# Shifting the starts of split weight parts and letting two PSUM banks take turns in a float32r decoder layer

## Chip, cores and metric

The kernel runs on one core of one Trainium2 chip. The metric is the device time of one execution in microseconds (us), the median of several runs.

## The reference

One hybrid decoder layer in float32 on 256 tokens of 2048 features. Cut to what matters:

```python
x = x + 0.5 * swiglu(rms_norm(x, g1), gate1, up1, down1)     # 2048 -> 5632 -> 2048
x = gated_parallel_mixer(x, ...)    # p = rms_norm(x) @ w_in; windowed attention and RWKV-7;
                                    # sigmoid gates; two projections; w_out
x = memory_cross_attention(x, mem, ...)
x = x + 0.5 * swiglu(rms_norm(x, g2), gate2, up2, down2)
return rms_norm(x, final)

def swiglu(h, w_gate, w_up, w_down):
    return (silu(h @ w_gate) * (h @ w_up)) @ w_down
```

Nearly all arithmetic is the product of 256 rows of tokens with weight matrices that are each read once.

## The kernel before

**Products.** `weight_plan` lists 105 products in their order; `EDGES` marks where the mixer (34) and the second feed-forward (71) begin. A product takes all 256 tokens against 512 columns of a weight matrix (288 in one case) and sums over its rows in chunks of 128. The tokens are two blocks of 128, so a product has two PSUM banks, `o[0]` and `o[1]`, from three rotating buffers named `acc`. A feed-forward works through three groups of columns (4, 4 and 3 times 512). Within a group gate and up products alternate, and then come four down products whose input is `h`. From product 71 on, the odd ones are all eleven gate products and six of the twelve down products.

**Split operands.** Each float32 operand is kept as two float32r parts, `hi` and `lo`, that add up to it, and each chunk costs three matmuls per bank: activation high part times weight `hi` (line 336), high part times weight `lo` (line 337), activation low part times weight `hi` (line 338). The activation chunk is the stationary operand (128x128, loaded by a LDWEIGHTS before each matmul), the weight part is the moving one (512 columns). The names after `<-` in the profile are moving, then stationary: `acc<-lo,xhi`.

**Units.** Weights are loaded by SyncE and split in units of two chunks (`KU`), twelve matmuls to a unit: six into `o[0]`, then six into `o[1]`. `divide` makes `hi` by a cast on ScalarE (line 299) and `lo` by a subtraction on VectorE (line 300), two units ahead of the multiplication (`AHEAD`), from loads that run further ahead. `hi` and `lo` have three buffers each, so the cast for unit u + 2 waits until TensorE has finished unit u - 1.

**Places.** The stationary operands are `xhi`/`xlo` (the normalised input of the feed-forwards and of most mixer products), `hhi`/`hlo` (the feed-forwards' inner activations) and the mixer's `ya`, `yr`, `mt`, `me` and `oc`. Where a tile begins within each partition follows from the allocation, in order of declaration in steps of 32 bytes. Taken modulo 128 bytes, all buffers of `hi` and `lo` begin at 96, `xhi` and `xlo` at 96, `hhi` and `hlo` at 64, and the mixer's tiles at 0, 32, 64 or 96 by their slot, since slots are 4128 bytes apart. Chunks and token blocks within a tile are multiples of 512 bytes apart.

**Order.** Between the steps of a product the `Interleave` object emits short steps of other work (transposes, norms, the mixer's attention and recurrence) by `bg.tick()`. A scheduler then orders each engine's instructions and sets the waits. The banks of a gate product are emptied by ScalarE (SiLU, line 415), those of an up product by VectorE (line 418), those of a down product by VectorE (line 427).

Of the kernel before, what the change touches and what calls it, by code (L numbers as in the profile page):

```python
# [15 lines left out]
P = 128  # L16
T = 256
# [10 lines left out]
KU = 2  # L28
# The decayed query-side factors carry 2^-40, the masks and the carried state 2^40: no product
# of a later key with an earlier query, which the masks remove, can overflow.  # L30
UP, DOWN = 2.0**40, 2.0**-40
GROUPS = ((0, 4), (4, 4), (8, 3))
N4 = 20
# Weight units whose split, and whose load, runs ahead of the one that is multiplied.
AHEAD, LOADED = 2, 4
# Products before the mixer, and before the second feed-forward.
EDGES = (34, 71)


class Act:  # L40
    """Activations with features on partitions, as two float32r parts that add up to them."""

# [8 lines left out]
class Interleave:  # L51
    """Short steps of other work, traced between the steps of the weight products."""

# [35 lines left out]
def weight_plan(a):  # L89
    """Every product with a weight matrix in its order: matrix, row chunk, chunks, column, columns."""  # L90
    w = {n: v[0] for n, v in a.items() if "_w_" in n or n.startswith("w_")}
    yield from feed_forward_plan(w["ffn1_w_gate"], w["ffn1_w_up"], w["ffn1_w_down"])
    w_in = w["w_in"]
    cols = [0, 512, ATTN_W]
    for c in cols:
        yield w_in, 0, KD, c, 512
    yield w_in, 0, KD, C_RW + 3 * RW, 288
    for h in range(2):
        yield w_in, 0, KD, C_RW + RW + h * 512, 512
    for n in range(4):  # L100
        yield w_in, 0, KD, C_GATE + n * 512, 512
        yield w["w_proj_attn"], 0, 8, n * 512, 512
    for h in range(2):
        yield w_in, 0, KD, C_RW + h * 512, 512
        yield w_in, 0, KD, C_RW + 2 * RW + h * 512, 512
    for n in range(4):
        yield w_in, 0, KD, C_GATE + D + n * 512, 512
    for n in range(4):
        yield w["w_proj_rwkv"], 0, 8, n * 512, 512
    for n in range(4):  # L110
        yield w["w_out"], 0, KD, n * 512, 512
    yield w["w_cross_kv"], 0, KD, 0, 512
    yield w["w_cross_q"], 0, KD, 0, 512
    yield w["w_cross_kv"], 0, KD, 512, 512
    for n in range(4):
        yield w["w_cross_o"], 0, 4, n * 512, 512
    yield from feed_forward_plan(w["ffn2_w_gate"], w["ffn2_w_up"], w["ffn2_w_down"])
# [3 lines left out]
def decoder_layer(ctx: ExitStack, tc: tile.TileContext, a: dict, out: bass.AP):  # L121
# [37 lines left out]

# [1 line left out]
    ones = cpool.tile([P, P], F32, name="ones")  # L161
# [9 lines left out]
    select(ident[:], ones[:], [[-1, P]], ALU.is_equal, 0.0, 0, 1)  # L171
    # attention bias: [previous block | current block], rows are queries
    abias = cpool.tile([P, 2, P], F32, name="abias")
    pool.memset(abias[:], 0.0)
    select(abias[:, 0, :], abias[:, 0, :], [[1, P]], ALU.is_gt, NEG, 0, -1)
    select(abias[:, 1, :], abias[:, 1, :], [[-1, P]], ALU.is_ge, NEG, 0, 1)
    # masks with the source step on partitions and the later step along the row
    ups = cpool.tile([P, P], F32, name="ups")
# [4 lines left out]
    select(mask3[:, 2, :], ups[:], [[1, P]], ALU.is_ge, 0.0, 0, -1)  # L183
    # with the later step on partitions
    mask_l = cpool.tile([P, P], F32, name="mask_l")
# [20 lines left out]

# [1 line left out]
    def row_vectors(rows, name, queue):  # L208
        """The vectors, and what fills them once their rows are there."""
        n = len(rows)  # L210
        r = cpool.tile([n, P], F32, name=name + "_r")
        at = 0
        while at < n:
            src, lo = rows[at]
            m = 1
            while at + m < n and rows[at + m][0] is src and rows[at + m][1] == lo + m * P:
                m += 1
            queue.dma_start(
                r[at : at + m, :], src[lo : lo + m * P].rearrange("(c p) -> c p", p=P)
            )  # L220
            at += m
        v = cpool.tile([P, n], F32, name=name)

        def fill():
            t = tr()
            pe.transpose(t[:, :n], r[:], ident[:n, :n])
            return act.copy(v[:], t[:, :n])

        return v, fill
# [36 lines left out]

# [1 line left out]
    plan = list(weight_plan(a))  # L268
# [5 lines left out]
    def load(u):  # L274
        """In the feed-forwards two units at once, into the pool of that phase."""
        if u >= len(units) or u in raws:
# [14 lines left out]
    def divide(u):  # L291
        if u >= len(units) or u in parts:
            return
        n, raw = units[u][3], raws[u]
        hi = wp.tile([P, KU, n], F32R, tag="hi", name="hi")
        lo = wp.tile([P, KU, n], F32R, tag="lo", name="lo")
        for s in (slice(0, 1), slice(1, 2)) if u == 0 else (slice(0, KU),):
# [14 lines left out]
    def product(x: Act, w, skew=False):  # L312
        """Rows of tokens: two [128, n] banks of x.T @ (the next columns of w)."""
        pw, _, nk, _, n = plan[at["product"]]
# [4 lines left out]
        for k in range(0, nk - KU * len(skewed), KU):  # L319
            bg.until(lambda: all(k + i in x.done for i in range(KU)))  # L320
            u = next_unit()
            for t in range(2):
                multiply(o[t][:, :n], x, u, k, t, nk)
                bg.tick()
        last = [(k, next_unit()) for k in skewed]
        for t in range(2):
            for k, u in last:
                multiply(o[t][:, :n], x, u, k, t, nk)
        return o

    def multiply(o, x, u, k, t, nk):
# [8 lines left out]
    def feat(tok, cols):  # L340
        """Token rows [128, 2, n] -> at up to two column offsets [128, 2, T] with features on
        partitions."""
        b = tr()
# [6 lines left out]
    def split(x: Act, c, n, src):  # L350
        """src (float32, PSUM or SBUF) -> chunks c to c + n of x."""
        act.copy(x.at(0, c, n), src)  # L352
        dve.tensor_tensor(x.at(1, c, n), src, f32(x.at(0, c, n)), ALU.subtract)
        x.done |= set(range(c, c + n))

# [1 line left out]
    class Norm:  # L357
# [8 lines left out]
        def block(self, n, src):  # L366
            """Steps for column block n of 512, src [128, 2, 512]; the last one ends the sums."""
            for h in range(2):
# [28 lines left out]

# [1 line left out]
    def feed_forward(sp, x, norm: Norm, wg, wu, wd, done, last=False):  # L399
# [41 lines left out]

    # ==== feed-forward 1 ====
    with tc.tile_pool(name="f1", bufs=1, reuse_waits="tile") as sp:
# [28 lines left out]

    # ==== token mixer and cross attention ====
    with tc.tile_pool(name="mx", bufs=1, reuse_waits="tile") as sp:
# [17 lines left out]

        # -- attention: a group of heads and a block of queries at a time --
        def to_features(tok, dst, name):
# [14 lines left out]
        def keys_values():  # L509
            # keys of each of the four heads on both halves of the partitions  # L510
            b = feat(tok_kv, C4[:2])
# [88 lines left out]

        # -- RWKV: columns with token shift, features on partitions --
        def shifted(tok, cols, mus, outs, name):
# [35 lines left out]
        def decay_and_rate():  # L638
# [28 lines left out]
            for h in range(2):  # L667
# [15 lines left out]
                act.activation(dec[h][:], dec[h][:], AF.Exp, scale=-DECAY)  # L683
                # decay from the middle of a chunk to each step, after that to the step before it
                ee.append(t4("ee", (P, 8, P + 1)))
# [10 lines left out]
        def removal_keys(h):  # L696
# [39 lines left out]
            pool.tensor_tensor(aa[h][:], kt[h][:], ei[:], ALU.mult)  # L736
            # products of the removal keys of later with those of earlier steps: L
            for c in range(2):
# [20 lines left out]

        # (1 - D)^-1 of the 32-step diagonal blocks, one block per partition  # L760
        def substitute():
# [27 lines left out]

        # -- the attention branch, gated --  # L790
        for n in range(4):
# [8 lines left out]

        # -- RWKV: receptances and values --
        rt, vtok, bv = [], [], []
# [15 lines left out]
        def values(h):  # L818
# [3 lines left out]
            for c in range(2):  # L822
                b = tr()
                # the recurrence keeps, and the group norm wants, values less their mean in a head
                for j in range(4):
# [16 lines left out]

        # -- RWKV: the two chunks of a pair of heads --
        xb = {}
# [121 lines left out]

        # -- group norm, bonus, gate, for two pairs --
        yr = Act([], [], 4)
# [53 lines left out]

        # -- the gate of the RWKV branch --
        for n in range(4):
# [5 lines left out]

        # -- merge and project out --
        mt = act_tiles("mt", 4)
# [38 lines left out]

        # -- cross attention --
        km, vm, qc = t4("km"), t4("vm", (P, 2, 512)), t4("qc")
# [68 lines left out]

    # ==== feed-forward 2 and the last norm ====
    with tc.tile_pool(name="f2", bufs=1, reuse_waits="tile") as sp:
# [69 lines left out]
```

## Time and profile before

| | |
|---|---|
| Time, median of 2 runs | 2351.23 us (2349.24 to 2353.22) |
| Span of the profiled execution | 2345.8 us |
| TensorE busy | 2323.1 us, 99% of the span, 10869 matmuls |
| Weight loads (beside the matmuls) | 1897.3 us, 81% |
| VectorE, ScalarE, GpSimd busy | 1256.9, 1075.6, 130.3 us |
| Memory traffic | 432.71 MB, 184 GB/s over the span |

The profile shows one execution, and its own time is given as its span; what lies around the span is the difference from the runs' median, 5.4 us. PE is TensorE's matmuls, PEld its weight loads, DVE VectorE, ACT ScalarE, POOL GpSimd and SP SyncE. A group's row ends in its busy time, the mean duration in ns and the idle time before it. The durations of matmuls overlap, so the pace of TensorE is read from the distance of their starts.

### The profile page before, as it was taken

What the parts mean: (1) busy time and instruction counts of PE and PEld (TensorE: products, weight loads), DVE (VectorE), ACT (ScalarE), POOL (GpSimd) and SP (SyncE); (2) the same over time, 40 slices, a digit from 0 to 9 for tenths busy, and PEclk for the clock granted to TensorE, in tenths of its full rate; (3) what the DMA queues carried; (4) which work ended last, traced back from release to release, by engine and by line L of the source; (5) the groups of instructions that cost most, each with busy time, mean ns of one, the idle gap of its engine ahead of it and who ended that gap; (6) DMA issues with size and microseconds to landing.
All of it is one profiled execution on the core that took longest, in us unless ns stands there. A gap on an engine that the chain in (4) does not pass through costs nothing.

```text
span 2345.8 us, 27378 instructions
## 1 busy us (share of the span) xinstructions
PE 2323.1 (99%) x10869; PEld 1897.3 (81%) x10869; DVE 1256.9 (54%) x1393; ACT 1075.6 (46%) x1425; POOL 130.3 (6%) x192
## 2 busy tenths in 40 slices
PE   8999999999999999999999999999999999999998
PEld 7888888888888877888888878888888888888886
DVE  5544444544555477795444456555545544544554
ACT  5443344433445477444344546455443344434444
POOL 1000000000000000201220030001000000000001
PEclk9999999999999999999999999999999999999999
DMA  8555556655554644676432576648555556555653
GB/s 288 182 194 183 194 185 192 190 187 188 188 188 145 177 128 146 211 224 200 118 99 84 182 246 218 192 161 290 186 193 184 187 190 195 183 190 187 197 180 126
DMA packets 219856, 432.71 MB, mean 184 GB/s; under 512 B 14267, under 2 KB 17040, under 8 KB 219728
## 3 DMA queue, kind: packets, MB, share of 16 engines
q1 hardware_dynamic: 211520, 405.58, 54.3%
q0 software_dynamic: 8176, 25.38, 3.4%
q8 instruction: 85, 1.39, 0.2%
q14 instruction: 43, 0.35, 0.0%
q10 hardware_dynamic: 32, 0.01, 0.0%
HBM read 417.56 MB, written 13.11 MB: 184 GB/s over the span
## 4 chain that ended last, share of the span: by engine, by line
PE 93%; issue 4%; DVE 1%; ACT 1%; DMA 1%; POOL 0%; SPq 0%; POOLq 0%; ACTq 0%
PE acc L336 28%; PE acc L338 28%; PE acc L337 28%; PE tr L347 2%; PE mm L925 1%; PE tr L893 1%; DMA raw<-in_ffn_w_gate_dram 0%; ACT hi L299 0%; PE mm L536 0%; POOL ml L1047 0%; PE tr L908 0%; PE tr L912 0%; PE tr L995 0%; DVE lo L300 0%; PE tr L575 0%
## 5 line engine op out<-in xcount | busy, mean ns | idle before, releaser
L300 DVE TENSOR_TENSOR lo<-raw,hi 128x1024 fp32r<-128x1024 f32 (+1 forms) x769 | 940.2, 1223 | 981.5 <-ACT hi L299 980.7
L299 ACT CAST hi<-raw 128x1024 fp32r<-128x1024 f32 (+1 forms) x769 | 802.5, 1044 | 1084.1 <-PE acc L338 1040.8
L336 PE MATMUL acc<-hi,xhi 128*128 128x512 f32 (+1 forms) x2016 | 798.6, 396 | 0.8 <-ACT xhi L373 0.5
L337 PE MATMUL acc<-lo,xhi 128*128 128x512 f32 (+1 forms) x2016 | 784.7, 389 | 0.3 <-DVE lo L300 0.3
L338 PE MATMUL acc<-hi,xlo 128*128 128x512 f32 (+1 forms) x2016 | 784.8, 389 | 0.0
L336 PEld LDWEIGHTS acc<-hi,xhi 128*128 128x128 f32 x2016 | 379.4, 188 | 81.1 <-issue 3.4
L337 PEld LDWEIGHTS acc<-lo,xhi 128*128 128x128 f32 x2016 | 379.4, 188 | 79.0 <-issue 3.3
L338 PEld LDWEIGHTS acc<-hi,xlo 128*128 128x128 f32 x2016 | 378.7, 188 | 79.3 <-issue 1.0
L336 PE MATMUL acc<-hi,hhi 128*128 128x512 f32 x704 | 280.6, 399 | 0.0
L338 PE MATMUL acc<-hi,hlo 128*128 128x512 f32 x704 | 279.1, 396 | 0.0
L337 PE MATMUL acc<-lo,hhi 128*128 128x512 f32 x704 | 279.0, 396 | 0.0
L338 PEld LDWEIGHTS acc<-hi,hlo 128*128 128x128 f32 x704 | 132.6, 188 | 32.3
L337 PEld LDWEIGHTS acc<-lo,hhi 128*128 128x128 f32 x704 | 132.7, 188 | 31.5
L336 PEld LDWEIGHTS acc<-hi,hhi 128*128 128x128 f32 x704 | 132.6, 188 | 31.4
L336 PE MATMUL acc<-hi,mthi 128*128 128x512 f32 x128 | 51.7, 404 | 0.0
L338 PE MATMUL acc<-hi,mtlo 128*128 128x512 f32 x128 | 50.6, 395 | 0.0
L337 PE MATMUL acc<-lo,mthi 128*128 128x512 f32 x128 | 50.4, 394 | 0.0
L1167 POOL TENSOR_TENSOR x<-x,fin 128x512 f32<-128x512 f32 x6 | 8.9, 1497 | 704.0 <-ACT junk L1165 704.0
L465 POOL DMA_DIRECT2D x1d<-x x4 | 3.0, 744 | 717.9 <-DVE x L427 717.9
L415 ACT ACTIVATE hb<-acc,rs 128x512 f32<-128x512 f32 x44 | 30.2, 691 | 19.6 <-PE acc L338 19.6
L352 ACT CAST hhi<-tr 128x512 fp32r<-128x512 f32 x44 | 25.7, 585 | 16.7 <-PE tr L347 16.7
L373 ACT ACTIVATE xhi<-tr,gains 128x256 fp32r<-128x256 f32 x48 | 22.0, 472 | 22.1 <-DVE xlo L374 16.2
(288 smaller groups left out, 1640.8 us busy)
## 6 DMA issues: line engine op xcount, KB each, us to landing
raw<-in_ffn_w_up_dram SPq DMA_DIRECT2D x88, 1024.0 KB, 5.2
raw<-in_ffn_w_down_dram SPq DMA_DIRECT2D x88, 1024.0 KB, 5.1
raw<-in_ffn_w_gate_dram SPq DMA_DIRECT2D x86, 1024.0 KB, 5.2
raw<-in_w_in_dram SPq DMA_DIRECT2D x136, 512.0 KB, 3.7
raw<-in_w_out_dram SPq DMA_DIRECT2D x32, 512.0 KB, 4.3
raw<-in_w_proj_attn_dram SPq DMA_DIRECT2D x16, 512.0 KB, 3.8
raw<-in_w_proj_rwkv_dram SPq DMA_DIRECT2D x16, 512.0 KB, 6.4
raw<-in_w_cross_kv_dram SPq DMA_DIRECT2D x16, 512.0 KB, 3.6
```

The lines of the kernel that those rows point to most:

```text
L299: act.copy(hi[:, s], raw[:, s])
L300: dve.tensor_tensor(lo[:, s], raw[:, s], f32(hi[:, s]), ALU.subtract)
L336: pe.matmul(o, xh, hi[:, i, :], start=k + i == 0, stop=False)
L337: pe.matmul(o, xh, lo[:, i, :], start=False, stop=False)
L338: pe.matmul(o, xl, hi[:, i, :], start=False, stop=k + i == nk - 1)
L347: pe.transpose(b[:, o : o + P], tok[:, t, col : col + P], ident[:])
L352: act.copy(x.at(0, c, n), src)
L373: last = act.activation(self.x.at(0, c), b[:, j, :], AF.Copy, scale=g)
L415: act.activation(hb[:, t, :], pg[t][:], AF.Silu, scale=norm.r[t])
L893: pe.matmul(b[e][:, m * P : (m + 1) * P], x1[r, j, cs_], x2[r, j, cs_], start=True, stop=True,)
L925: pe.matmul(vb[:, (o + e) * P : (o + e + 1) * P], lhs(e), rhs[:], start=first and e == 0, stop=True, **ek,)
L1167: pool.tensor_tensor(xs, xs, fin[:, n * 512 : (n + 1) * 512], ALU.mult)
```

## The change

Each buffer of `hi` and `lo` gets 32 more elements (128 bytes), and the part begins inside it at a place that depends on the unit's number u: `hi` at 16·(u mod 8) bytes, `lo` at 16·((u div 8) mod 8) bytes. In every fourth block of 64 units 8 bytes are added, except to the eighth place. In the second feed-forward each odd product multiplies a chunk into both banks in turn, part by part, instead of a unit's six matmuls into one bank and then six into the other. Comments and docstrings are dropped as well.

```diff
     def divide(u):
...
-        hi = wp.tile([P, KU, n], F32R, tag="hi", name="hi")
-        lo = wp.tile([P, KU, n], F32R, tag="lo", name="lo")
+        fine = 2 if u // 64 % 4 == 3 else 0
+
+        def part(name, step):
+            t = wp.tile([P, KU * n + 32], F32R, tag=name, name=name)
+            o = 4 * (step % 8) + (fine if step % 8 < 7 else 0)
+            return t[:, o : o + KU * n].rearrange("p (a n) -> p a n", a=KU)
+
+        hi, lo = part("hi", u), part("lo", u // 8)
...
             u = next_unit()
+            if alternate(at["product"] - 1):
+                for i in range(KU):
+                    crossed(o, x, u, k, i, nk, n)
+                    bg.tick()
+                continue
             for t in range(2):
                 multiply(o[t][:, :n], x, u, k, t, nk)
                 bg.tick()
...
+    def alternate(i):
+
+        return i >= EDGES[1] and i % 2 == 1
+
+    def crossed(o, x, u, k, i, nk, n):
+        hi, lo = u
+        for which in range(3):
+            for t in range(2):
+                xp = x.at(1 if which == 2 else 0, k + i)[:, t * P : (t + 1) * P]
+                w = lo if which == 1 else hi
+                pe.matmul(
+                    o[t][:, :n], xp, w[:, i, :], start=k + i == 0 and which == 0,
+                    stop=which == 2 and k + i == nk - 1,
+                )
```

In the scheduled order only TensorE's sequence changes, in the 17 odd products. In the first unit of 16 of them the second bank is touched by the third matmul; before, it was the seventh.

## The prediction

> **What bounds the kernel now.** I read the page first: span, busy shares, the granted clock and the chain that ended last.
>
> ```profile
> span 2345.8 us, 27378 instructions
> ...
> PE 2323.1 (99%) x10869; PEld 1897.3 (81%) x10869; DVE 1256.9 (54%) x1393; ACT 1075.6 (46%) x1425; POOL 130.3 (6%) x192
> ...
> PEclk9999999999999999999999999999999999999999
> ...
> PE 93%; issue 4%; DVE 1%; ACT 1%; DMA 1%; POOL 0%; SPq 0%; POOLq 0%; ACTq 0%
> ```
>
> TensorE is busy for 99% of the span at the full clock, and 93% of the chain is TensorE. So the time is the number of matmuls times the step from one matmul's start to the next. Next I read the groups of instructions for how many weight matmuls there are and which tile is the stationary operand (the second name after `<-`). Lines 337 and 338 have the same counts as line 336.
>
> ```profile
> L336 PE MATMUL acc<-hi,xhi 128*128 128x512 f32 (+1 forms) x2016 | 798.6, 396 | 0.8 <-ACT xhi L373 0.5 <-ACT hb L415 0.2
> ...
> L336 PE MATMUL acc<-hi,hhi 128*128 128x512 f32 x704 | 280.6, 399 | 0.0
> ...
> L336 PE MATMUL acc<-hi,mthi 128*128 128x512 f32 x128 | 51.7, 404 | 0.0
> ...
> L336 PE MATMUL acc<-hi,mehi 128*128 128x512 f32 x64 | 25.9, 405 | 0.0
> L336 PE MATMUL acc<-hi,yrhi 128*128 128x512 f32 x64 | 25.8, 403 | 0.0
> ...
> L336 PE MATMUL acc<-hi,yahi 128*128 128x512 f32 x64 | 25.0, 391 | 0.0
> ...
> L336 PE MATMUL acc<-hi,ochi 128*128 128x512 f32 x32 | 13.3, 416 | 0.0
> ```
>
> A weight unit is twelve matmuls (four of each line), so there are 2016/4 = 504 units against `x`, 704/4 = 176 against `h`, and (128 + 64 + 64 + 64 + 32)/4 = 88 against the mixer's tiles: 768 units.
>
> Third, ScalarE's timeline, for the step itself. A cast of line 299 needs a `hi` buffer that TensorE frees once per unit, so in undisturbed stretches the casts beat time for twelve matmuls. The first three rows are against `x`, the next three against `h`, then three against `mt`, then two against `yr`.
>
> ```profile
> 1906.77 1.05 ACT L299 CAST hi<-raw 128x1024 fp32r<-128x1024 f32 x1 [1.67 <-PE acc L338]
> 1909.49 1.05 ACT L299 CAST hi<-raw 128x1024 fp32r<-128x1024 f32 x1 [1.67 <-PE acc L338]
> 1912.21 1.05 ACT L299 CAST hi<-raw 128x1024 fp32r<-128x1024 f32 x1 [1.67 <-PE acc L338]
> ...
> 1804.01 1.05 ACT L299 CAST hi<-raw 128x1024 fp32r<-128x1024 f32 x1 [1.75 <-PE acc L338]
> 1806.83 1.05 ACT L299 CAST hi<-raw 128x1024 fp32r<-128x1024 f32 x1 [1.76 <-PE acc L338]
> 1809.64 1.05 ACT L299 CAST hi<-raw 128x1024 fp32r<-128x1024 f32 x1 [1.76 <-PE acc L338]
> ...
> 1484.15 1.05 ACT L299 CAST hi<-raw 128x1024 fp32r<-128x1024 f32 x1 [1.72 <-PE acc L338]
> 1486.94 1.05 ACT L299 CAST hi<-raw 128x1024 fp32r<-128x1024 f32 x1 [1.74 <-PE acc L338]
> 1489.74 1.05 ACT L299 CAST hi<-raw 128x1024 fp32r<-128x1024 f32 x1 [1.74 <-PE acc L338]
> ...
> 1353.85 1.05 ACT L299 CAST hi<-raw 128x1024 fp32r<-128x1024 f32 x1 [1.70 <-PE acc L338]
> 1356.62 1.05 ACT L299 CAST hi<-raw 128x1024 fp32r<-128x1024 f32 x1 [1.72 <-PE acc L338]
> ```
>
> The same twelve matmuls with the same moving tiles take 2.72 us against `x` (226.7 ns each), 2.81 against `h` (234.2), 2.79 to 2.80 against `mt` and 2.77 against `yr`. Only the stationary tile differs. Its place within 128 bytes differs too: `hi`, `lo`, `xhi` and `xlo` all begin at remainder 96, `hhi` and `hlo` at 64, and the mixer's tiles at 0, 32, 64 and 96 in mixed company. The fastest stage is the one in which stationary and moving tiles begin at the same remainder. That is my reading of the rows: the step depends on where the two reads of TensorE stand to each other.
>
> **The change, part by part.** Only TensorE's order changes, and only inside 17 products of the second feed-forward. ScalarE, VectorE, GpSimd and SyncE run the same instructions in the same order, with the same loads and stores on the same queues. The padding moves every later tile by 768 bytes, six times 128, so `h` and the mixer's tiles keep their remainders, and `x` does not move at all.
>
> *The starts.* In unit u, `hi` now begins 16·(u mod 8) bytes further on and `lo` 16·(u div 8 mod 8), with 8 bytes more in every fourth block of 64 units. So no stage keeps its relation: 63 of 64 combinations differ from the one that `x` has now, and equally few are like that of `h`. Each product runs through all eight places of `hi`. The nearest rows for a stage of changing relations are those of the mixer's tiles, whose parts stand at several remainders: 2.77 to 2.80. I take 2.78 per unit. Then `x` costs 504 x (2.78 - 2.72) = +30.2 us, `h` 176 x (2.78 - 2.81) = -5.3 us, and the rest nothing: +24.9 us, all on the path, since TensorE has no cover.
>
> No row has an operand at an odd multiple of 16 bytes or at 8. The bounds come from the shortest and longest undisturbed matmul in any stage (min/median/max in ns, in the view of the instructions that use `hi`; the 290 of `x` belongs to its 288-column form, and the maxima of 628 and 482 hold waits, so the longest is taken from `h`):
>
> ```profile
> L338 PE MATMUL acc<-hi,xlo x2016: 290/389/628, 10.5 to 2268.5; 128*128 128x512 f32 x181, 128*128 128x288 f32 x3
> ...
> L338 PE MATMUL acc<-hi,hlo x704: 391/397/403, 192.7 to 2336.9; 128*128 128x512 f32 x176
> ...
> L338 PE MATMUL acc<-hi,mtlo x128: 387/394/482, 1398.1 to 1494.9; 128*128 128x512 f32 x128
> ```
>
> These durations follow the step: 397 - 389 = 8 ns between `h` and `x`, against 7.5 ns by the casts. The shortest, 387, is 2 ns under `x`'s median, a step of 224.7 ns or 2.70 us per unit; the longest, 403, is 14 ns above it, 240.7 ns or 2.89 us. With m us per unit on average, the change is 768 m - (504 x 2.72 + 176 x 2.81 + 88 x 2.78) = 768 m - 2110.1: -37 us at 2.70 and +109 us at 2.89.
>
> The Trainium skill speaks against my reading: SBUF — State Buffer, Who interferes with whom, gives TensorE two independent read ports, one for the moving operand and one for the weight load, and says that TensorE never waits on anyone. By that rule the starts would be free and the sum nearly zero. The trace disagrees, with 2.72 against 2.81 us for the same work.
>
> *ScalarE and VectorE* write and read at the shifted places. A cast takes 1.05 us and then idles 1.67 in each 2.72; the subtraction (below) takes 1.23. Unit u + 2 is cast about 0.2 us after unit u begins (the row of 1912.21 against the matmul of 1912.01, below). The cast of 1909.49 is followed by the subtraction of 1910.57, over at 1911.80, 2.5 us after its unit u began; the first read of that `lo` comes two units and one matmul after that beginning, 2 x 2.72 + 0.23 = 5.7 us. So 3.2 us hide this; only if cast and subtraction together grew from 2.3 to 5.5 us would TensorE wait. Cost: nothing.
>
> *Taking turns.* The 17 products hold 11 x 96 + 4 x 96 + 2 x 72 = 1584 matmuls, 132 units. The number of matmuls and weight loads is unchanged. What a change of bank costs, and what stands at the end of a product, is here:
>
> ```profile
> 1889.09 0.69 ACT L415 ACTIVATE hb<-acc,rs 128x512 f32<-128x512 f32 x1 [0.31 <-PE acc L338]
> 1890.45 0.69 ACT L415 ACTIVATE hb<-acc,rs 128x512 f32<-128x512 f32 x1 [0.67 <-PE acc L338]
> ...
> 1910.57 1.23 DVE L300 TENSOR_TENSOR lo<-raw,hi 128x1024 fp32r<-128x1024 f32 x1 [1.50 <-ACT hi L299]
> ...
> 1911.71 1.40 DVE L418 SCALAR_TENSOR_TENSOR hb<-acc,rs,hb 128x512 f32<-128x512 f32 x2
> 1911.78 0.39 PE L338 MATMUL acc<-hi,xlo 128*128 128x512 f32 x1
> ...
> 1912.01 0.39 PE L336 MATMUL acc<-hi,xhi 128*128 128x512 f32 x1
> ...
> 1912.24 0.39 PE L337 MATMUL acc<-lo,xhi 128*128 128x512 f32 x1
> ...
> 1912.46 0.39 PE L338 MATMUL acc<-hi,xlo 128*128 128x512 f32 x1
> ```
>
> From 1911.78 to 1912.01 the bank changes, from 1912.01 to 1912.24 it doesn't: 0.23 us both. So alternation itself is worth nothing either way. At the border into such a product, the second bank is the one that the product before left first. Its eviction is the first half of the 1.40 us pair, over at about 1912.41. Now that bank is needed by the third matmul, at 1912.46, instead of the seventh. A hand-over of 0.2 us (the cast at 1912.21 against the matmul that freed it, over when the next began at 1912.01) leaves TensorE waiting 0.15 us; 16 such borders give 2.4 us, and none if the hand-over is quicker. I take 2. Queued behind that matmul are TensorE's own, and nobody else is late. At the far border both banks end together, so ScalarE's two activations (0.69 us each) run back to back, the first done 0.9 us after the end; the next product wants that bank six matmuls, 1.36 us, after it. The cast behind them starts 0.7 us later, out of those 3.2 us. No cost, while that slack lasts.
>
> The Trainium skill has a rule against this too: TensorE: Matmul & The Clock Gate, A second HAM failure mode: psum-queue depth-cycling, tells of a kernel that cycled through banks, idled in short pauses and lost clock for it. The trace grants the full clock over the whole stage with its bank changes:
>
> ```profile
> 1700.00:2300.00 600.00, 600.00 (x2654) 491.94 (x2653) 298.49 (x270) 248.09 (x255) 2.94 (x2) 1.00 0.58 188
> ```
>
> *Sum:* 24.9 + 2 = +27 us on a span of 2345.8, so 2373. The page gives only the span; the median of the two runs shown, 2351.2, lies 5.4 us above, which I carry over: 2378 us, +1.1%.
>
> **The rivals.** (A) The starts don't matter to TensorE, or only the stationary tile's own place does, which is not changed: 2351.2 + 2 = 2353. For it: all moving tiles start at one remainder now, so the rows can't separate "relation" from "stationary place". Against it: nothing that I can price.
>
> (B) Slower: the new places are as bad as `h`'s or worse. Half of all starts are odd multiples of 16 bytes, in all three stages, and 192 units have 8 bytes more; if the mean is 2.81, the 504 units of `x` lose 45.4 us and the mixer's 2.6: with the border 2401. At the longest row, 2.89, it is +111: 2462. It decides over 2% from 768 m - 2110.1 + 2 = 47, m = 2.806. For it: `h` is a uniform relation and shows that a single bad one can persist. Against it: the mixer's mixed relations stay below that, and `yr` at 2.77.
>
> (C) Faster: with all moving tiles at one remainder each matmul may wait for its turn to start, and shifted starts break this up. At the shortest row, 2.70, it is -37 + 2: 2316. Beyond 2% it must come to m = 2.68 (223.7 ns), which no row shows; against it too is that `x`, whose places agree, is already the fastest stage. The Trainium skill's page TensorE: Matmul & The Clock Gate, Back-to-back issue gap, has 216 ns for 512 columns in bf16; by that all units would take 2.59 us and the time would be some 2232 (an estimate from that page).
>
> (D) The alternating products idle and lose the clock: at half clock 132 units take another 132 x 2.78 = 367 us, 2720. Against it: the last two fences.
>
> **How the numbers follow.** My forecast, 2378, has 0.50; its own range is 2.76 to 2.80 per unit, +10 to +40 us, with the border 2363 to 2394. A has 0.14, B 0.24, C 0.09, D 0.03. About 2% (47 us) is what a measurement of this kernel can tell from no change. Within it lie the forecast, A and 0.02 of C: 0.66. Slower by more: B and D, 0.27. Faster by more: 0.07, the part of C that goes past the shortest row. The range takes in C at its row price and B to past its middle: 2310 to 2440; outside stay 0.07 of C, 0.03 of D and some 0.06 of B.
>
> **What would show it right or wrong.** Right: casts against `x` no longer evenly 2.72 us apart but mostly 2.75 to 2.82, changing with u mod 8 and with the block of eight; casts against `h` below 2.81 on average; alternating products no different from their neighbours but for 0.15 us at their start; clock 1.00; busy times of lines 299 and 300 as before. Wrong: `x` still at 2.72 (A), a mean of 2.81 and more or long matmuls in the blocks with 8 bytes more (B), steps under 224 ns (C), a clock below 1 in the second feed-forward (D), or a wait of TensorE for `lo` or for an eviction beyond 0.2 us.

## The result, and the profile after

| | Before | Changed |
|---|---|---|
| Median of 2 runs | 2351.23 us | 2373.32 us (2371.42 to 2375.22) |
| Ratio | | 1.0096, 95% interval 1.0067 to 1.0125 |
| Span of the profiled execution | 2345.8 us | 2373.5 us |

The changed kernel is 1.0% slower, inside the 2% that count as no change here, and 4.7 us below the forecast of 2378. The page of the changed kernel (first parts; the chain; the groups of the split):

```profile
span 2373.5 us, 27378 instructions
...
PE 2351.8 (99%) x10869; PEld 1900.4 (80%) x10869; DVE 1259.8 (53%) x1393; ACT 1074.4 (45%) x1425; POOL 130.2 (5%) x192
...
PEclk9999999999999999999999999999999999999999
...
PE 93%; issue 4%; DMA 1%; DVE 1%; ACT 1%; POOL 0%; SPq 0%; POOLq 0%; ACTq 0%
...
L306 DVE TENSOR_TENSOR lo<-raw,hi 128x1024 fp32r<-128x1024 f32 (+1 forms) x769 | 941.9, 1225 | 1000.3 <-ACT hi L305 997.0
L305 ACT CAST hi<-raw 128x1024 fp32r<-128x1024 f32 (+1 forms) x769 | 801.8, 1043 | 1102.5 <-PE acc L364 877.6
```

The split's two groups in the page of the kernel before:

```profile
L300 DVE TENSOR_TENSOR lo<-raw,hi 128x1024 fp32r<-128x1024 f32 (+1 forms) x769 | 940.2, 1223 | 981.5 <-ACT hi L299 980.7
L299 ACT CAST hi<-raw 128x1024 fp32r<-128x1024 f32 (+1 forms) x769 | 802.5, 1044 | 1084.1 <-PE acc L338 1040.8
```

TensorE still fills 99% of the span with as many matmuls as before. The span grew by 27.7 us and TensorE's busy time by 28.7 (2351.8 - 2323.1). The split costs ScalarE and VectorE what it did (801.8 and 941.9 us of busy time, 802.5 and 940.2 before): they wait longer, ScalarE for TensorE and VectorE for ScalarE. So it is the step of the matmul. ScalarE's timeline of the changed kernel shows it, first in an alternating product against `x`, then at the end of one against `h` (releaser line 352) and in the ordinary product behind it (364):

```profile
1940.38 1.05 ACT L305 CAST hi<-raw 128x1024 fp32r<-128x1024 f32 x1 [1.70 <-PE acc L352]
1943.17 1.05 ACT L305 CAST hi<-raw 128x1024 fp32r<-128x1024 f32 x1 [1.75 <-PE acc L352]
1945.97 1.05 ACT L305 CAST hi<-raw 128x1024 fp32r<-128x1024 f32 x1 [1.74 <-PE acc L352]
1948.76 1.05 ACT L305 CAST hi<-raw 128x1024 fp32r<-128x1024 f32 x1 [1.74 <-PE acc L352]
...
1817.02 1.05 ACT L305 CAST hi<-raw 128x1024 fp32r<-128x1024 f32 x1 [1.71 <-PE acc L352]
1819.79 1.05 ACT L305 CAST hi<-raw 128x1024 fp32r<-128x1024 f32 x1 [1.73 <-PE acc L352]
1822.57 1.05 ACT L305 CAST hi<-raw 128x1024 fp32r<-128x1024 f32 x1 [1.73 <-PE acc L352]
1825.34 1.05 ACT L305 CAST hi<-raw 128x1024 fp32r<-128x1024 f32 x1 [1.73 <-PE acc L364]
1828.12 1.05 ACT L305 CAST hi<-raw 128x1024 fp32r<-128x1024 f32 x1 [1.73 <-PE acc L364]
```

Twelve matmuls against `x` now take 2.79 to 2.80 us instead of 2.72; against `h` they take 2.76 to 2.78 instead of 2.81, whether the banks alternate or not. For the whole execution I use one figure per stage: the mean distance between the starts of neighbouring weight matmuls of 512 columns, of all distances under 300 ns, worked out from the trace. It is called the step below.

| Step, ns | against `x` | against `h` | mixer's tiles |
|---|---|---|---|
| Before | 227.2 | 234.2 | 231.3 |
| Changed | 232.2 | 232.2 | 232.4 |
| Matmuls | 6048 | 2112 | 1056 |
| Difference, us | +30 | -4 | +1 |

The matmuls against `x` include 96 of 288 columns. With about 1 us at the borders of the alternating products (below) this is 28 us, against the spans' 27.7.

That the two meet so closely is in part luck. In the profiled execution of the changed kernel the granted clock (the third figure from the end) stood at half in two stretches of 3.4 us in the mixer; in the same windows of the execution before it is 1.00:

```profile
874.40:877.80 3.40, 3.40 (x13) 2.19 (x13) 1.75 (x2) 1.85 (x4) 0.00 (x0) 0.50 0.89 240
905.10:908.50 3.40, 3.40 (x10) 2.27 (x9) 3.33 (x6) 3.25 (x6) 0.00 (x0) 0.50 0.53 154
```

At half the clock they cost some 2 x 1.7 = 3.4 us. They belong to the execution and not to the change: the profiled execution of the starts alone (below) has none, that of the turns alone has three. Without them the change costs 27.7 - 3.4 = 24.3 us. The steps overshoot this by 3 to 4 us, since the table charges the longer step to every matmul: some 250 of those against `x` have 288 columns or stand before another kind of matmul, and some 160 distances of 300 ns and more hold waits, which take up part of the longer step.

### The profile page after: what moved, and what is told of

Same layout as the page of the kernel before. It is cut to its first block, busy times and chain, and to the rows that moved or that the text cites. A ratio compares the mean times of both kernels' runs of the same rounds, so it can differ in the third digit from the quotient of the medians.

```text
span 2373.5 us, 27378 instructions
## 1 busy us (share of the span) xinstructions
PE 2351.8 (99%) x10869; PEld 1900.4 (80%) x10869; DVE 1259.8 (53%) x1393; ACT 1074.4 (45%) x1425; POOL 130.2 (5%) x192
## 4 chain that ended last, share of the span: by engine, by line
PE 93%; issue 4%; DMA 1%; DVE 1%; ACT 1%; POOL 0%; SPq 0%; POOLq 0%; ACTq 0%
PE acc L362 23%; PE acc L363 23%; PE acc L364 23%; PE acc L352 15%; PE tr L373 2%; PE mm L951 1%; PE tr L919 1%; DMA raw<-in_ffn_w_up_dram 1%; ACT hi L305 0%; PE mm L562 0%; DVE lo L306 0%; POOL ml L1073 0%; PE tr L934 0%; PE tr L938 0%; PE tr L601 0%
## 5 line engine op out<-in xcount | busy, mean ns | idle before, releaser
L306 DVE TENSOR_TENSOR lo<-raw,hi 128x1024 fp32r<-128x1024 f32 (+1 forms) x769 | 941.9, 1225 | 1000.3 <-ACT hi L305 997.0
L305 ACT CAST hi<-raw 128x1024 fp32r<-128x1024 f32 (+1 forms) x769 | 801.8, 1043 | 1102.5 <-PE acc L364 877.6
L362 PE MATMUL acc<-hi,xhi 128*128 128x512 f32 (+1 forms) x1664 | 668.7, 402 | 0.0
L363 PE MATMUL acc<-lo,xhi 128*128 128x512 f32 (+1 forms) x1664 | 655.6, 394 | 0.2 <-DVE lo L306 0.2
L364 PE MATMUL acc<-hi,xlo 128*128 128x512 f32 (+1 forms) x1664 | 654.7, 394 | 0.0
L364 PE MATMUL acc<-hi,hlo 128*128 128x512 f32 x528 | 208.1, 394 | 0.0
L364 PEld LDWEIGHTS acc<-hi,hlo 128*128 128x128 f32 x528 | 99.3, 188 | 23.4
L363 PEld LDWEIGHTS acc<-lo,hhi 128*128 128x128 f32 x528 | 99.4, 188 | 22.7
L362 PEld LDWEIGHTS acc<-hi,hhi 128*128 128x128 f32 x528 | 99.2, 188 | 22.6
L352 PE MATMUL acc<-hi,xhi 128*128 128x512 f32 x352 | 114.5, 401 | 0.0
L352 PE MATMUL acc<-lo,xhi 128*128 128x512 f32 x352 | 112.0, 394 | 0.0
L352 PE MATMUL acc<-hi,xlo 128*128 128x512 f32 x352 | 110.7, 395 | 0.0
L352 PEld LDWEIGHTS acc<-hi,xlo 128*128 128x128 f32 x352 | 66.2, 188 | 15.5
```

Source lines behind the costliest of these rows:

```text
L305: act.copy(hi[:, s], raw[:, s])
L306: dve.tensor_tensor(lo[:, s], raw[:, s], f32(hi[:, s]), ALU.subtract)
L352: pe.matmul(o[t][:, :n], xp, w[:, i, :], start=k + i == 0 and which == 0, stop=which == 2 and k + i == nk - 1,)
L362: pe.matmul(o, xh, hi[:, i, :], start=k + i == 0, stop=False)
L363: pe.matmul(o, xh, lo[:, i, :], start=False, stop=False)
L364: pe.matmul(o, xl, hi[:, i, :], start=False, stop=k + i == nk - 1)
```

## The experiments

Each ratio is to the kernel before on the same chip, with its 95% interval.

**The turns alone.** Line 352 is `crossed`; the tiles of `hi` and `lo` stay as before:

```diff
+            if alternate(at["product"] - 1):
+                for i in range(KU):
+                    crossed(o, x, u, k, i, nk, n)
+                    bg.tick()
+                continue
```

> The alternating of banks alone, with all parts at their old places. Theory (the whole change in time is in the starts; turns are worth 0 to 2.4 us): 2351 to 2354 us, units against x at 2.72 us and against h at 2.81, in alternating products as in their neighbours. Rival (the turns cost or save something that the shifted starts hide or cause): more than 5 us away from 2351, and alternating products with another unit time than their neighbours.

Measured: 2352.37 us, ratio 1.0009 [0.9999, 1.0019]. In the view of the instructions that use `hi` (min/median/max ns), line 358 is the ordinary order and 346 the alternating one:

```profile
L358 PE MATMUL acc<-hi,xlo x1664: 290/389/632, 10.4 to 2275.5; 128*128 128x512 f32 x181, 128*128 128x288 f32 x4
L346 PE MATMUL acc<-hi,xlo x352: 389/389/481, 1603.8 to 2253.8; 128*128 128x512 f32 x176
...
L346 PE MATMUL acc<-hi,hlo x176: 392/397/400, 1784.6 to 2327.1; 128*128 128x512 f32 x176
```

The medians are the same in both orders, 389 against `x` and 397 against `h`. From its first weight matmul to its last the second feed-forward takes 740.6 us in this trace and 738.5 in that of the kernel before. So the turns cost the 2 us of the forecast (the ratio's interval allows 0 to 4.5 us), and the rest of the change's time is in the starts.

**The starts alone.** The change without the turns:

```diff
     def alternate(i):
 
-        return i >= EDGES[1] and i % 2 == 1
+        return False
```

> The shifted starts alone, products in the old order. Theory: the same time as the changed kernel, 2371 to 2375 us (its 2373.3 less at most 2.4), units near 2.78 us in all three stages. Rival (the turns are part of the loss): nearer to 2351 by more than 5 us.

Measured: 2373.9 us, ratio 1.0102 [1.0087, 1.0117]; steps 232.1, 232.1 and 232.5 ns. As far as the times can tell, that is the whole change. Its profiled execution, without a stretch at half clock, has a span of 2369.5 us, 23.7 above the 2345.8 of the kernel before.

**Every part moved by 96 bytes.** If only the two starts' relation within 128 bytes counts, this should have exchanged the fates of `x` and `h`:

```diff
-        hi = wp.tile([P, KU, n], F32R, tag="hi", name="hi")
-        lo = wp.tile([P, KU, n], F32R, tag="lo", name="lo")
+        def part(name, o):
+            t = wp.tile([P, KU * n + 32], F32R, tag=name, name=name)
+            return t[:, o : o + KU * n].rearrange("p (a n) -> p a n", a=KU)
+
+        hi, lo = part("hi", 24), part("lo", 24)
```

> No sweep: hi and lo all begin 96 bytes further on, at remainder 64 of 128, as h does, while x stays at 96. Theory (the relation of moving to stationary place sets the step): the stages swap. Against h the unit takes 2.72 us, 176 x 0.09 = 16 us less; against x, which then stands 32 bytes above the moving tiles, no row of before has the exact relation in a uniform stage, so 2.77 to 2.81, 504 x 0.05 to 0.09 = 25 to 45 us more; 2360 to 2382 us. Rival 1 (the place of the stationary tile alone): nothing moves, x 2.72, h 2.81, 2351 us. Rival 2 (what counts is only that moving places do not change from matmul to matmul): the same 2351 us.

Measured: 2377.39 us, ratio 1.0119 [1.0104, 1.0134]; step against `x` 233.3, against `h` 231.1 ns. The same view:

```profile
L342 PE MATMUL acc<-hi,xlo x2016: 289/397/628, 10.4 to 2298.4; 128*128 128x512 f32 x181, 128*128 128x288 f32 x3
```

`x` became as bad as `h` had been (397), but `h` did not become as good as `x` had been (226.7 expected). The time lies in the range that was expected of the theory, but without the exchange on which that range rested. So the reading by 128 bytes, on which the prediction stood, is not right as it was put.

**A survey of places, buffers 128 bytes longer.** Every product gets one steady pair of shifts; `owner` gives a unit's product:

```diff
+        p = owner[u]
+        s = p % 8
+        d = 0 if p < EDGES[0] else 1 if p < EDGES[1] else 4
+        hi, lo = part("hi", 4 * s), part("lo", 4 * ((s + d) % 8))
```

> Starts that stay the same through a whole product and change from product to product: 16 times the product's number mod 8, for hi and lo alike in the first feed-forward, lo 16 bytes further in the mixer and 64 bytes further in the second feed-forward. Theory (relation, with a period of 128 bytes): in the first feed-forward the unit against x is 2.72 us in products with shift 0 and between 2.75 and 2.82 in the others; against h it is 2.72 us in products with shift 96 (which puts the moving tiles at h's remainder) and 2.81 with shift 0; x with shift 32 behaves as h with shift 0. Where hi and lo differ by 64, no product has 2.72. Rival 1 (stationary place alone): 2.72 in all products against x, 2.81 in all against h. Rival 2 (a change from unit to unit is what costs): all products near 2.72 or at their old pace, since nothing changes within one.

Measured: 2368.05 us in one run. The products of shift 0 against `x` in the first feed-forward, which by 128 bytes should have kept 226.7, had 230.7 to 231.4 ns on average. That points at the padding itself: buffers of 4224 bytes are 16.5 times 256 apart, so neighbours stand 128 bytes apart within 256, where the old 4096 bytes put all at one place. By the tiles' addresses `hi`, `lo` and `x` of the kernel before all begin at 224 modulo 256, and `h` at 64.

**The padding alone**, no part shifted:

```diff
-        hi, lo = part("hi", 24), part("lo", 24)
+        hi, lo = part("hi", 0), part("lo", 0)
```

> The padding alone: every hi and lo buffer is 128 bytes longer and begins at its old remainder of 128, with no shift and no turns. The old theory (relation modulo 128 bytes) says 2349 us, x at 2.72. The new theory (relation modulo 256 bytes: two buffers that follow each other are then 128 bytes apart modulo 256) says that the padding does nearly all of it: units against x at 2.77 to 2.78 and against h at 2.77 to 2.79, 2364 to 2374 us.

Measured: 2366.89 us, ratio 1.0074 [1.0059, 1.0089]; steps 231.2, 232.5 and 232.0 ns. ScalarE's timeline of this kernel, against `x`:

```profile
1935.58 1.05 ACT L303 CAST hi<-raw 128x1024 fp32r<-128x1024 f32 x1 [1.68 <-PE acc L342]
1938.35 1.05 ACT L303 CAST hi<-raw 128x1024 fp32r<-128x1024 f32 x1 [1.72 <-PE acc L342]
1941.12 1.05 ACT L303 CAST hi<-raw 128x1024 fp32r<-128x1024 f32 x1 [1.73 <-PE acc L342]
```

2.77 us, without one shifted start. Some three quarters of the loss (0.0074 of 0.0102) come with 128 unused bytes per buffer. It also explains the missing exchange: with 96 bytes added, buffers at 224 and 96 come to stand at 64 and 192, so one part of each pair agrees with `h` modulo 256 and the other does not, as here with `x`, and the steps are alike, 231.1 and 231.2 ns.

**A survey with buffers 256 bytes longer**, so that they all agree modulo 256 again, and places chosen in steps up to 240:

```diff
-            t = wp.tile([P, KU * n + 32], F32R, tag=name, name=name)
+            t = wp.tile([P, KU * n + 64], F32R, tag=name, name=name)
...
-        hi, lo = part("hi", 4 * s), part("lo", 4 * ((s + d) % 8))
+        hi, lo = (part(m, o // 4) for m, o in zip(("hi", "lo"), places[owner[u]]))
```

> Padding of 256 bytes, so that all buffers agree modulo 256, and shifts that stay the same through a product. New theory (modulo 256): against x the step of one matmul settles at 226.7 ns where hi and lo are shifted by 0, and at no other shift up to 240, 128 among them; against h at 226.7 where both are shifted by 96 (224 + 96 is h's 64 modulo 256) and at 234.3 where both are shifted by 0; where only one of the two parts agrees, between 228 and 234. Rival (a longer period, 512 to 4096 bytes): 226.7 nowhere against h at 96. Rival (the equal distance of the buffers counts, not the relation): every equal pair of shifts settles, each at a value of its own, and 226.7 comes at other shifts too.

Measured: 2372.51 us in one run. ScalarE's timeline of this kernel, first two products against `h`, with both parts shifted by 96 (which puts them at 64, as `h`), then by 224; after that two products against `x`, unshifted and then both shifted by 128:

```profile
205.77 1.05 ACT L318 CAST hi<-raw 128x1024 fp32r<-128x1024 f32 x1 [1.67 <-PE acc L357]
208.49 1.05 ACT L318 CAST hi<-raw 128x1024 fp32r<-128x1024 f32 x1 [1.67 <-PE acc L357]
211.21 1.05 ACT L318 CAST hi<-raw 128x1024 fp32r<-128x1024 f32 x1 [1.67 <-PE acc L357]
...
227.76 1.05 ACT L318 CAST hi<-raw 128x1024 fp32r<-128x1024 f32 x1 [1.75 <-PE acc L357]
230.56 1.05 ACT L318 CAST hi<-raw 128x1024 fp32r<-128x1024 f32 x1 [1.75 <-PE acc L357]
233.36 1.05 ACT L318 CAST hi<-raw 128x1024 fp32r<-128x1024 f32 x1 [1.75 <-PE acc L357]
...
775.63 1.05 ACT L318 CAST hi<-raw 128x1024 fp32r<-128x1024 f32 x1 [1.67 <-PE acc L357]
778.35 1.05 ACT L318 CAST hi<-raw 128x1024 fp32r<-128x1024 f32 x1 [1.67 <-PE acc L357]
781.07 1.05 ACT L318 CAST hi<-raw 128x1024 fp32r<-128x1024 f32 x1 [1.67 <-PE acc L357]
...
795.77 1.05 ACT L318 CAST hi<-raw 128x1024 fp32r<-128x1024 f32 x1 [1.75 <-PE acc L357]
798.57 1.05 ACT L318 CAST hi<-raw 128x1024 fp32r<-128x1024 f32 x1 [1.75 <-PE acc L357]
```

2.72 us where both parts begin at the stationary tile's place modulo 256, and 2.80 us 128 bytes away from it, for `h` as for `x`. Settled steps from the trace, by the parts' distance from the stationary tile modulo 256:

| Distance of both parts | Step, ns |
|---|---|
| 0 (against `x` and against `h`) | 226.7 |
| 128 | 232.5 to 233.3 |
| other multiples of 16 | 228.9 to 236.7 |
| 0 for one part only | 228.9 to 235.6 |

No place was below 226.7. Both rivals fall: against `h` the step is 226.7 at a shift of 96, and no other equal pair of shifts has it. Where one part alone agrees the steps reach 235.6, beyond the 234 expected. Away from 0 the distance does not settle the step alone: 240 gave 236.7 against `x` and 233.3 against `h`. The Trainium skill's page SBUF — State Buffer, section Who interferes with whom, says that TensorE's moving read and its weight load have independent ports and that TensorE never waits on anyone. These runs differ from what one would expect by it: nothing but the places of TensorE's own two operands makes 2.72 or 2.80 us.

**`h` brought into step.** The kernel before with one unused tile of 160 bytes ahead of the pools that hold `h`, which moves `h` from 64 to 224 modulo 256; the weight parts are as before:

```diff
+    gap = stat.tile([P, 40], F32, tag="gap", name="gap", bufs=1)
+    pool.memset(gap[:], 0.0)
```

> The kernel before with one unused tile of 160 bytes ahead of the phases' pools, which moves h from 64 to 224 modulo 256, where x, hi and lo begin. New theory: units against h go from 2.81 to 2.72 us, 176 x 0.09 = -16 us; the mixer's tiles change places among themselves, -3 to +3 us; 2330 to 2337 us against 2349 to 2351, a ratio of 0.992 to 0.995. Rival (a longer period): h stays away from 2.72, the ratio is 0.998 to 1.002.

Measured: 2336.61 us, ratio 0.9947 [0.9934, 0.9959]; step against `h` 226.9 ns instead of 234.2, against `x` 227.2, in the mixer 232.1. Its rows for `hi`:

```profile
L338 PE MATMUL acc<-hi,hlo x704: 388/389/398, 192.6 to 2325.9; 128*128 128x512 f32 x176
L338 PE MATMUL acc<-hi,mtlo x128: 388/396/480, 1394.7 to 1491.5; 128*128 128x512 f32 x128
```

The median against `h` went from 397 to 389 ns, as against `x`. The steps account for 2112 x 7.3 = 15.4 us of gain less 1056 x 0.8 = 0.8 us lost in the mixer, 14.6 us, at the upper end of what the ratio's interval allows (9.6 to 15.5 us). The profiled executions agree with the steps: this one has two stretches at half clock and a span of 2334.8 us, without them 2331.4, which is 14.4 under the 2345.8 of the kernel before.

**The change's starts in buffers that agree modulo 256.** As the starts alone, with 64 elements of padding instead of 32.

> The change's shifts without its turns, in tiles padded by 256 bytes in place of 128, so that the buffers agree modulo 256 and the shifts alone break the relation. New theory: the shifts do it by themselves too, units of 2.76 to 2.79 in all stages, 2366 to 2376 us. Rival (the distance of the buffers is the whole cause): nearer to 2349 us by more than 10.

Measured: 2374.37 us, ratio 1.0104 [1.009, 1.0118]; steps 232.0 and 232.2 ns against `x` and `h`. So the shifted starts break the agreement by themselves too; padding and starts don't add up, since the agreement can be lost only once.

**Every stationary tile in step.** `h` as above; in the mixer, `ee` gets two slots of its own, and the shared pool has 18 slots instead of 20, so that its tiles all begin at 224 modulo 256:

```diff
-N4 = 20
+N4 = 18
...
-                ee.append(t4("ee", (P, 8, P + 1)))
+                ee.append(sp.tile([P, 8, P + 1], F32, tag="ee", name="ee", bufs=2))
```

> As the kernel with h in step, and the mixer's tiles too: the one larger tile among them, ee, gets two slots of its own (18 + 2 in place of 20), so that all others are 4096 bytes apart and begin at 224 modulo 256. New theory: the 88 units against the mixer's tiles go from 2.77-2.80 to 2.72 us, another 4 to 7 us less than the 2336.6 of h in step, 2329 to 2334 us, a ratio of 0.991 to 0.994. Rival (fewer slots make the mixer's work wait): the same or more than 2336.6 us, with waits for slots in the mixer.

Measured: 2332.74 us, ratio 0.9924 [0.9911, 0.9938]; steps 227.2, 226.9 and, in the mixer, 227.6 ns. The row for `mt` and ScalarE's timeline in its stage:

```profile
L338 PE MATMUL acc<-hi,mtlo x128: 388/389/478, 1393.6 to 1489.1; 128*128 128x512 f32 x128
...
1484.07 1.05 ACT L299 CAST hi<-raw 128x1024 fp32r<-128x1024 f32 x1 [1.66 <-PE acc L338]
1486.79 1.05 ACT L299 CAST hi<-raw 128x1024 fp32r<-128x1024 f32 x1 [1.67 <-PE acc L338]
1489.51 1.06 ACT L299 CAST hi<-raw 128x1024 fp32r<-128x1024 f32 x1 [1.67 <-PE acc L338]
```

2.72 us there too, where the kernel before had 2.79 to 2.80. The steps give 15.4 + 1056 x 3.7 ns = 19.3 us, within the interval's 14.6 to 20.9. So this version is faster than the kernel before by 0.8%, and than the changed one.

**The starts without the 8 bytes.** `fine = 0`, and no turns:

> The 16-byte starts alone, without the 8 bytes in every fourth block of 64 units and without turns. In the changed kernel the blocks with 8 bytes show steps of 233.3 ns on average, the others 231.9. If the 8 bytes are the reason, all blocks stand near 231.9 and the time is 2016 x 1.4 = 3 us less than with starts only: 2369 to 2372 us. Rival (these blocks are slower for their place in the plan): the same difference remains and the time is 2372 to 2375 us.

Measured: 2371.39 us, ratio 1.009 [1.0076, 1.0103]. In the trace with the 8 bytes (the starts alone) the three blocks that have them stand at 233.3 ns and the rest at 231.8; without them those three stand at 231.7 to 232.0 and the rest still at 231.8. So the 8 bytes cost 1.5 ns per matmul in their blocks, 192 x 12 x 1.5 ns = 3.5 us. The times alone don't resolve it, since the two intervals overlap.

## Why the prediction was right, and the step that wasn't

- **The bound held.** TensorE sets the time, at the full clock but for a few short stretches in the mixer, and the change is worth the matmuls times the difference of their step.
- **The price of the starts held.** I took 2.78 us per unit from the mixer's rows; 232.2 ns x 12 is 2.79. The term for `x` was +30.2 us and by the steps +30; for `h` -5.3 and -4; for the mixer 0 and +1. Together the starts were put at +24.9 us; by two executions without a stretch at half clock they cost 23.7. Rivals A (the starts don't matter), B (2.81 on average) and C (steps under 224 ns) all fell by this one figure.
- **The border held for the turns alone and was mis-sized, within its bounds, for the changed kernel.** I took 2 us between 0 and 2.4, and the turns alone cost 2.1 (740.6 - 738.5). TensorE's and VectorE's timeline of the changed kernel at such a border:

```profile
1933.29 1.40 DVE L444 SCALAR_TENSOR_TENSOR hb<-acc,rs,hb 128x512 f32<-128x512 f32 x2
...
1933.63 0.39 PE L352 MATMUL acc<-hi,xhi 128*128 128x512 f32 x1
...
1933.86 0.40 PE L352 MATMUL acc<-lo,xhi 128*128 128x512 f32 x1
1934.08 0.19 PEld L352 LDWEIGHTS acc<-hi,xhi 128*128 128x128 f32 x1 [0.27 <-DVE hb L444]
1934.09 0.49 PE L352 MATMUL acc<-hi,xhi 128*128 128x512 f32 x1
1934.42 0.39 PE L352 MATMUL acc<-lo,xhi 128*128 128x512 f32 x1
```

  The wait is where the prediction put it, but short: the matmul of 1934.09 is followed 0.33 us later instead of 0.23. Over the 14 borders whose rows are whole the excess is 0.8 us, about 1 us for 16. Against the starts alone, 746.9 us for the second feed-forward, the changed kernel takes 747.9.
- **Alternation itself cost nothing, and the clock stayed.** Rival D is out: the second feed-forward's row of the changed kernel has the clock at 1.00.

```profile
1700.00:2300.00 600.00, 600.00 (x2621) 484.61 (x2621) 295.34 (x267) 243.04 (x249) 0.00 (x0) 1.00 0.57 186
```

  The same stretch holds 2621 matmuls instead of 2654, 1.2% fewer, which is the longer step and about 1 us at the borders. What the Trainium skill tells of a kernel that cycled through banks and lost clock in short pauses (TensorE: Matmul & The Clock Gate, A second HAM failure mode: psum-queue depth-cycling) did not happen here: the clock is 1.00 in this stretch.
- **The sum was some 2 us too high, and the 5.4 us carried over are not what lies around the span.** The span was forecast at 2373 and is 2373.5, but 3.4 us of that are the two stretches at half clock. The change was put at +27 us; without them it is 24.3: the starts cost 23.7 instead of 24.9, and the borders about 1 instead of 2. In the changed kernel's two runs time and span differ by 1.7 us (2375.22 and 2373.5, 2371.42 and 2369.7). The other 3.7 of the 5.4 us are the scatter of executions, which goes with the clock: in the later experiments the kernel before has spans of 2344.9 to 2348.0 us at a mean granted clock of 0.999 and of 2348.3 to 2351.6 at 0.997. The rest of the 4.7 us by which the forecast missed lies within that scatter, since each median is of two runs.
- **The step that failed is the period.** I wrote that the step depends on the relation within 128 bytes, that 63 of 64 combinations differ from `x`'s, and that the padding, six times 128, keeps every remainder. Relation was right, 128 was not: it is 256, and both parts have to agree. The 768 bytes are three times 256 too, so the later tiles do stay; but the parts' own buffers come to stand 128 bytes apart. By the tiles' addresses not one of the changed kernel's 760 units of 512 columns has both parts in step with its stationary tile. The remainders of the mixer's tiles hid this: modulo 128 their slow rows stand "in mixed company" either way. So the padding alone already costs 1.0074, which the prediction had at nothing; the sum came out because padding and starts lose the same agreement, whose price I had from a row. That was partly luck: the mixer's rows happened to mix places modulo 256 as the change does. Nor does each product run through all eight places of `hi`, as I wrote: those of 4, 8 and 12 chunks do not, which changes no term of the sum.

What stays open: whether the moving read or the weight load is held up (the weight loads last 186 to 188 ns at the shortest and the median in the traces of both kernels; no run separates the two reads), why the step settles at 226.7 ns and not lower, what sets the step out of agreement, and what starts the stretches at half clock.

## What to carry to other kernels

When TensorE is full, read the distance between the starts of its matmuls stage by stage: two stages with the same matmuls and different steps differ in something that can be mended, here the place of the stationary tile against the moving one. In this kernel a pad of 128 bytes per buffer cost 0.7%, and an unused tile of 160 bytes elsewhere gained 0.5%, so on such a kernel look at what a new tile does to every later tile's place modulo 256. Before two spans are compared to a few us, look at the granted clock of both executions. A price taken from the nearest row can be right although the rule behind it is wrong; only the run that takes the rule at its word (here the shift by 96 bytes) tells them apart.

## What the runs showed of the hardware

- Matmuls of 512 float32r columns step at 226.7 ns when the stationary tile and both moving tiles begin at the same place modulo 256 bytes, and at 228.9 to 236.7 ns otherwise, at the same clock. 16-byte steps matter, and 8 bytes more cost another 1.5 ns on average in the changed kernel's blocks that have them.
- The settled steps in the survey stand mostly at 226.67, 228.89, 231.11, 232.22 and 233.33 ns, a few above. In the trace of before seven steps against `h` repeat every 1640 ns (238, 230, 235, 235, 233, 232, 237 ns). That looks like matmuls that wait for the next turn of something, but no run here shows what turns.
- From about 830 to 910 us, in the mixer, the traces hold from no stretch (before, starts alone) to three (turns alone) of 3.4 us at a granted clock of 0.50. With three of them the six products there took 162.8 us instead of 157.8.
